# Dealing rows to partitions so that the DMA engines of one core work on neighbouring blocks of DRAM

## The chip, the cores and the metric

One NeuronCore of one Trainium2 chip runs the kernel; the other cores are idle. The metric is the time of one execution in device microseconds. Runs of the kernel before lie within 3725.8 to 3726.7 us.

## The reference

A residual add and an RMS norm over 65536 rows of 2048 float32:

```python
batch, seq, dim = 32, 2048, 2048
z = x + residual
rms = np.sqrt(np.mean(z ** 2, axis=-1, keepdims=True) + eps)
return (z / rms * gamma).astype(np.float32)
```

It reads two arrays of 537 MB and writes one of 537 MB.

## The kernel before

The 65536 rows go through SBUF in 74 tiles: one of 128 x 3 rows, one of 128 x 5, then 72 of 128 x 7. A tile costs three transfers, all issued from the SP queue: load the residual (`r_area`), load x (`z`), store the result (`out`, from `z`). Partition p holds 7 rows that follow one another in DRAM, a block of 56 KiB.

```python
    def rows(t, i):
        k = sizes[i]
        return t[starts[i] : starts[i] + P * k, :].rearrange("(p r) m -> p r m", r=k)
    # ... cut ...
    def load_x(sp, t, d=0):
        i = t.i + d
        inc(sp.dma_start(out=z[i % 2][:, : sizes[i], :], in_=rows(x_f, i)), "x_in", i)
    # ... load_r: the same with r_area and r_f; cut ...
    def sp_turn(sp, t):
        i = t.i
        t.wait(sp, "done", -1)                  # tile i-1 is scaled
        inc(sp.dma_start(out=rows(o_f, i - 1), in_=z[(i - 1) % 2][:, : sizes[i - 1], :]),
            "s_out", i - 1)
        # ... cut ...
        t.wait(sp, "add_a")                     # first part of the add of tile i is done
        load_r(sp, t, 1)
        t.wait(sp, "s_out", -1)                 # the store has landed, its z is free
        # ... the last tile is loaded in four pieces; cut ...
        load_x(sp, t, 1)
```

VectorE adds and scales, ScalarE squares and sums; both work on whole partitions and don't care which rows a partition holds.

## Time and profile before

| | before |
|---|---|
| time | 3726.47 us median of 4 (3725.92 to 3726.7) |
| bytes moved | 1610.66 MB, 432 GB/s over the span |
| a packet of 56 KiB on one DMA engine | 2.116 to 2.128 us from fastest to 99th per cent |
| VectorE, ScalarE busy | 62%, 29% |

The page's lines stand in the prediction below, with how they are read. A packet is one engine's copy of one contiguous run; here, one partition's block. The packet durations come from the trace's packet records, which hold start, length and size, but neither engine nor address. So which engine serves which partitions is nowhere recorded. The engines are numbered here by the group that they serve; their own numbers are not in the records.

### The profile page before, as it was taken

Reading aid. Unit: us, or ns where it says so; the run is one execution under the profiler, and the core shown is the slowest. Engines: PE = TensorE matmul, PEld = TensorE weight load, DVE = VectorE, ACT = ScalarE, POOL = GpSimd, SP = SyncE. Lnnn points to the kernel's source line nnn. Section 1 sums busy time; section 2 is a strip of 40 time slices with the busy share of each in tenths; the row PEclk is TensorE's granted clock in tenths of the full one; section 3 lists DMA queues with packets and bytes.
Section 4 is the critical chain, followed back from the end, with each engine's and each line's share of the span. In section 5 each row is a group of like instructions: output and inputs, shape, how many; then the busy total and the mean of one; then the engine's idle time right before and its main releaser. Section 6 shows DMA issues by size and latency. Waiting matters only on the chain.

```text
span 3724.7 us, 3652 instructions
## 1 busy us (share of the span) xinstructions
DVE 2302.5 (62%) x816; ACT 1072.4 (29%) x1176; POOL 0.2 (0%) x4
## 2 busy tenths in 40 slices
DVE  5666665566665566665566665566665566655566
ACT  2233322233322233322233322233322233322233
POOL 0000000000000000000000000000000000000000
DMA  9999999999999999999999999999999999999999
GB/s 420 432 434 434 434 434 434 432 434 434 435 434 434 434 434 436 434 434 434 433 434 434 434 434 434 434 434 434 434 434 434 434 434 434 434 434 434 434 434 398
DMA packets 32964, 1610.69 MB, mean 432 GB/s; under 512 B 3712, under 2 KB 3776, under 8 KB 3776
## 3 DMA queue, kind: packets, MB, share of 16 engines
q1 hardware_dynamic: 32960, 1610.66, 99.9%
q14 instruction: 4, 0.03, 0.0%
HBM read 1073.77 MB, written 536.87 MB: 432 GB/s over the span
## 4 chain that ended last, share of the span: by engine, by line
DMA 66%; DVE 22%; issue 9%; ACT 2%; SPq 0%; DVEq 0%; ACTq 0%
DMA out_dram<-z 33%; DMA z<-in_x_dram 33%; DVE z L170 15%; DVE z L175 7%; ACT sq_junk L221 1%; DMA r_area<-in_gamma_dram 0%; ACT rms L229 0%; DVE rstd L195 0%; DVEq L126 0%; SPq L255 0%; DVE r_area L274 0%; ACTq L209 0%; ACTq L126 0%; DVE tail_rstd L291 0%; SPq L160 0%
## 5 line engine op out<-in xcount | busy, mean ns | idle before, releaser
L170 DVE TENSOR_TENSOR z<-z,r_area 128x8192 f32<-128x8192 f32 (+2 forms) x150 | 1109.4, 7437 | 1253.2 <-DMA z<-in_x_dram 1227.6
L221 ACT ACTIVATE sq_junk<-z 128x2048 f32<-128x2048 f32 x512 | 963.4, 1882 | 2618.1 <-DVE z L170 2606.7
L175 DVE SCALAR_TENSOR_TENSOR z<-z,rstd,gamma_tile 128x2048 f32<-128x2048 f32 x505 | 1153.5, 2344 | 5.2
L195 DVE RECIPROCAL rstd<-rms 128x4 f32<-128x4 f32 (+2 forms) x146 | 25.3, 173 | 130.8 <-ACT rms L229 130.8
L221 ACT ACTIVATION_READ_ACCUMULATOR sq_junk<-z 128x1 f32 x512 | 95.4, 186 | 0.0
L229 ACT ACTIVATE rms<-ssq,eps_tile 128x4 f32<-128x4 f32 (+2 forms) x146 | 43.3, 297 | 13.4
L175 DVE SCALAR_TENSOR_TENSOR z<-z,tail_rstd,gamma_tile 128x2048 f32<-128x2048 f32 x7 | 16.2, 2346 | 0.1
L276 DVE LOAD_MASK_SELECT gamma_tile<-r_area x1 | 0.0, 14 | 16.4 <-DMA r_area<-in_gamma_dram 16.4
L276 DVE STREAM_SHUFFLE gamma_tile<-r_area 128x2048 f32<-128x2048 f32 x1 | 2.3, 2290 | 0.0
L274 DVE MEMSET r_area<- 128x2048 f32 x1 | 1.8, 1765 | 0.4 <-issue 0.4
L221 ACT ACT_TABLE_LOAD x1 | 1.3, 1283 | 0.9 <-SPq L75 0.9
L229 ACT ACT_TABLE_LOAD x1 | 1.3, 1283 | 0.1
L229 ACT ACTIVATE tail_rms<-tail_ssq,eps_tile 128x2 f32<-128x2 f32 (+1 forms) x4 | 1.2, 296 | 0.1
L273 DVE MEMSET eps_tile<- 128x1 f32 x1 | 0.1, 59 | 1.0 <-SPq L75 1.0
L291 DVE RECIPROCAL tail_rstd<-tail_rms 128x2 f32<-128x2 f32 (+1 forms) x4 | 0.6, 158 | 0.0
L348 POOL MEMSET const-bfloat16-1.0<- 128x1 bf16 x1 | 0.1, 102 | 0.0
L348 POOL MEMSET const-uint8-127<- 128x1 uint8 x1 | 0.1, 102 | 0.0
L348 POOL MEMSET const-float32-1.0<- 128x1 f32 x1 | 0.1, 99 | 0.0
L348 POOL MEMSET const-float32-0.0<- 128x1 f32 x1 | 0.1, 98 | 0.2 <-issue 0.2
## 6 DMA issues: line engine op xcount, KB each, us to landing
r_area<-in_residual_dram SPq DMA_DIRECT2D x72, 7168.0 KB, 27.2
z<-in_x_dram SPq DMA_DIRECT2D x71, 7168.0 KB, 33.8
out_dram<-z SPq DMA_DIRECT2D x71, 7168.0 KB, 34.5
z<-in_x_dram SPq DMA_DIRECT2D x3, 2048.0 KB, 26.3
out_dram<-z SPq DMA_DIRECT2D x3, 2048.0 KB, 13.9
r_area<-in_residual_dram SPq DMA_DIRECT2D x1, 5120.0 KB, 25.3
z<-in_x_dram SPq DMA_DIRECT2D x1, 5120.0 KB, 36.8
out_dram<-z SPq DMA_DIRECT2D x1, 5120.0 KB, 24.7
```

Source lines behind the costliest of these rows:

```text
L170: return v.tensor_add(out=s, in0=s, in1=r_area[:, e + a : e + b, :])
L175: ins = v.scalar_tensor_tensor(out=s, in0=s, scalar=rs[:, c + g - a : c + g - a + 1], in1=gamma_tile[:, :], op0=mult, op1=mult,)
L195: v.reciprocal(out=rstd[p][h][:, :n], in_=rms[p][h][:, :n]).then_inc(dve, U)
L221: s.activation(out=sq_junk[:, :], in_=src[:, g, :], func=Act.Square, accum_out=sq[:, g - a : g - a + 1],)
L229: return s.activation(out=rm, in_=sq[:, : b - a], func=Act.Sqrt, bias=eps_tile[:, :], scale=inv_d)
L273: v.memset(eps_tile[:, :], float(eps))
L274: v.memset(stage, 0.0).then_inc(tail_ev["add"], 1)
L276: v.stream_shuffle(gamma_tile[:, :].rearrange("p (a b) -> p a b", a=16), stage, [0] * 32)
L291: v.reciprocal(out=tail_rstd[:, a:b], in_=tail_rms[:, a:b]).then_inc(dve, U)
L348: nc = _bacc.Bacc("TRN2", target_bir_lowering=False, num_devices=1)
```

## The change

The intent: while the 16 DMA engines work through a transfer, they should be on neighbouring blocks of DRAM. The rows of a tile are dealt so that block number 16j + e goes to partition 8e + j; if engine e serves partitions 8e to 8e+7, the 16 engines start on blocks 0 to 15, then go on to 16 to 31.

```diff
     def rows(t, i):
         k = sizes[i]
-        return t[starts[i] : starts[i] + P * k, :].rearrange("(p r) m -> p r m", r=k)
+        t = t[starts[i] : starts[i] + P * k, :]
+        return t.rearrange("(j e r) m -> e j r m", e=16, r=k)
# ... cut: two index expressions for the pieces of the last tile get one more dimension
```

Loads and stores use the same `rows`, so every row comes back to its place.

More of the change, by code (lines that the diff above doesn't have):

```diff
@@ L160, in sp_turn @@
                 sp.dma_start(
-                    out=z[last % 2][:, a:b, :], in_=rows(x_f, last)[:, a:b, :]
+                    out=z[last % 2][:, a:b, :], in_=rows(x_f, last)[:, :, a:b, :]
                 ).then_inc(x_tail[k], U)
@@ L265, in sync_program @@
             sp.dma_start(
-                out=rows(o_f, last)[:, a:b, :], in_=z[last % 2][:, a:b, :]
+                out=rows(o_f, last)[:, :, a:b, :], in_=z[last % 2][:, a:b, :]
             ).then_inc(s_tail, U)
```

## The prediction

The point is 6300 us, with a range of 3780 to 7480 us: 1.7 x 3711 + 15 = 6324, where 3711 us is the bytes at the measured 434 GB/s and 15 us is start and end. 2 for a pair of engines in step (2 x 2.12 = 4.24 us a packet) and 1.7 as the centre stand as estimates. A pair means two engines that hold each other up; that there are such pairs p1 shows, further below.

> **What bounds the kernel now.** I read the page from the top: busy engines, the slices, the queue, then the groups with their idle time, then the waits of the queue that issues the transfers, and last one stretch of the chain of waits.
>
> The busy shares and the slices (40 equal stretches of the span, DMA being the mean busy tenths of the 16 engines):
>
> ```profile
> span 3724.7 us, 3652 instructions
> ...
> DVE 2302.5 (62%) x816; ACT 1072.4 (29%) x1176; POOL 0.2 (0%) x4
> ...
> DMA  9999999999999999999999999999999999999999
> GB/s 420 432 434 434 434 434 434 432 434 434 435 434 434 434 434 436 434 434 434 433 434 434 434 434 434 434 434 434 434 434 434 434 434 434 434 434 434 434 434 398
> ...
> q1 hardware_dynamic: 32960, 1610.66, 99.9%
> ```
>
> No compute engine is near full, and the 16 DMA engines are busy for 99.9% of the span. Except in the first and last slice the rate stands at 434 GB/s, flat. [...] Per engine it is 434 / 16 = 27.1 GB/s. The bytes alone take 1610.66 MB / 434 GB/s = 3711 us, which leaves about 15 us of the 3726.35 us for start and end.
>
> Who waits (groups: busy and mean, then idle time before and its releaser) and what one transfer takes:
>
> ```profile
> L170 DVE TENSOR_TENSOR z<-z,r_area 128x8192 f32<-128x8192 f32 (+2 forms) x150 | 1109.4, 7437 | 1253.2 <-DMA z<-in_x_dram 1227.6
> ...
> r_area<-in_residual_dram SPq DMA_DIRECT2D x72, 7168.0 KB, 27.2
> z<-in_x_dram SPq DMA_DIRECT2D x71, 7168.0 KB, 33.8
> out_dram<-z SPq DMA_DIRECT2D x71, 7168.0 KB, 34.5
> ```
>
> VectorE's only large idle time is for x to land. A 7 MiB transfer needs 7.34 MB / 434 GB/s = 16.9 us of service, yet lands 27 to 34.5 us after issue: it stands in the ring behind about one whole other transfer. So the rings don't run dry. A stretch of the chain of waits in the middle of the run (start, length, what) says the same, two transfers' time per link:
>
> ```profile
> 978.42 34.42 DMA out_dram<-z
> ...
> 1012.86 33.81 DMA z<-in_x_dram
> ```
>
> A tile is three transfers, 50.8 us, against 2302.5/75 = 31 us of VectorE. The bound is the rate at which 16 DMA engines pass bytes, and nothing else has a say.
>
> How the bytes are cut: 228 of the 232 transfers carry tiles. 228 x (128 + 16) = 32832, plus four small gamma loads of 16 + 16 packets, is exactly 32960. So each partition's run of a tile (7 rows, 56 KiB) is one packet, 8 per engine and transfer, and each engine adds one completion write. In the trace's packet records a 56 KiB packet takes 2.116 to 2.128 us from the fastest to the 99th per cent, that is 27.1 GB/s, whether it is a read or a write of DRAM.
>
> [...]
>
> **The change part by part.** No computation changes, nor the number of transfers, their bytes or the waits. The listing of the built program against the old one shows only the shapes of the transfers moved: where both sides had 128 rows of 14336 elements, the DRAM side is now 16 x 8 x 14336 and the SBUF side 128 x 1 x 14336. Runs stay 56 KiB long, so 128 + 16 packets per transfer stay.
>
> Removed on the DRAM side: distance. I expect this to be worth nothing. If each engine is at a fixed 27.1 GB/s, DRAM is not what it waits for. [...]
>
> Added on the SBUF side, and not intended: [...]
>
> Its cost in lockstep: [...] a packet 4.24 us instead of 2.12, a 7 MiB transfer 33.9 us instead of 16.9, the run 2 x 3711 + 15 = 7437 us. Compute at 31 us a tile hides under 101 us.
>
> What softens it: [...] So the size hangs on the lag within pairs. In the landing records of the kernel before, the 16 landings of one transfer lie 0.9 to 1.1 us apart from first to last in the first 100 us, and mostly 3.3 to 4.7 us later. In packets of 2.12 us that is 0.5 at first and 1.6 to 2.2 later, for the most distant engines; a pair is usually closer. [...] I take 1.7 as the centre: 1.7 x 3711 + 15 = 6324, rounded to 6300 us.
>
> Issue of a transfer takes 0.33 us on the queue's sequencer in the timeline; a three-dimensional shape may take longer. Even 0.3 us more over 228 issues is 68 us, but beside at least 17 us of queued transfers it is hidden, so 0.
>
> **The rivals.**
>
> (1) Nothing happens: [...] The time would be 3726 give or take 10 us.
>
> (2) The pairs unlock themselves: [...] The time would be near 3750 to 4000. [...]
>
> (3) DRAM gains: a rate over 434 GB/s. Against: the ceiling above[...].
>
> (4) Neighbouring blocks make DRAM slower, all 16 engines being close together. I give it little. It would show as slow packets with no doubling pattern.
>
> **Range and chances.** Full lockstep is the upper end, 7437[...]. The lower end, 3780, holds most of the self-unlocking case but not the nothing-happens case. I give 16% to within 2% (rival 1, and a quick complete unlocking), 1% to faster, 83% to slower. Within slower, about a sixth lies below 4300, the rest spread from 5000 to 7450. The point is the middle of an uneven distribution, not a sharp value.
>
> **What would show it.** Right: the same 32960 packets and 1610.66 MB on the queue, DMA still at 9 in every slice (engines count as busy while blocked), GB/s well under 434, packets of 56 KiB taking between 2.12 and 4.24 us with many near the upper value, landings of 7 MiB loads stretched by the same factor, busy times of VectorE and ScalarE unchanged in us but a smaller share. GB/s rising along the span would show lag building up. Wrong: 434 GB/s throughout[...], packets longer than 4.3 us[...] (DRAM), or DMA share falling below 9 with the queue's waits on issue grown (issue cost).

## The result, and the profile after

The changed kernel takes 7070.9 us, median of 4 (7038.2 to 7098.18), against 3726.47 us. The ratio is 1.8972, with a 95% interval of 1.8868 to 1.9075. Ratios here are the mean time of one kernel's fast runs over that of the other's of the same rounds, so not quite the ratio of the medians quoted.

The page of the changed kernel, in the parts that answer to those of before: busy engines, slices, queue, the group that waits, and the transfers with their median time to landing.

```profile
span 7044.8 us, 3652 instructions
...
DVE 2302.6 (33%) x816; ACT 1072.4 (15%) x1176; POOL 0.2 (0%) x4
...
DMA  9999999999999999999999999999999999999999
GB/s 227 239 233 228 234 232 234 231 232 225 229 231 228 228 227 223 229 229 230 229 222 226 228 229 228 225 222 228 229 229 228 223 228 229 230 229 225 223 228 241
...
q1 hardware_dynamic: 32960, 1610.66, 99.7%
...
L171 DVE TENSOR_TENSOR z<-z,r_area 128x8192 f32<-128x8192 f32 (+2 forms) x150 | 1109.4, 7437 | 4544.6 <-DMA z<-in_x_dram 4544.6
...
r_area<-in_residual_dram SPq DMA_DIRECT2D x72, 7168.0 KB, 56.6
z<-in_x_dram SPq DMA_DIRECT2D x71, 7168.0 KB, 68.4
out_dram<-z SPq DMA_DIRECT2D x71, 7168.0 KB, 91.8
```

Packets and bytes are the same to the last one, and so is what VectorE and ScalarE do, in us. What changed is that the engines, busy as before (99.7%), pass half as much: 229 GB/s. Busy here means that an engine has a packet open, not that it moves bytes at its full rate; only GB/s beside the busy share shows the difference. VectorE's wait for x grew from 1228 to 4545 us, by 3317 us, which is nearly the whole of the added 3344 us. The rate is flat from the first slice to the last. The median landing times did not stretch by one factor: 2.08 and 2.02 times for the two loads, 2.66 times for the store.

In the packet records the mean packet of 56 KiB went from 2.118 to 4.012 us. The distribution between 1000 and 3000 us of the run:

```
                before      after
under 2.2 us      100%         7%
2.2 to 4.1 us       0%        18%
over 4.1 us         0%        75%   (median of all 4.30, 90th per cent 4.47)
```

The timeline shows an issue of a transfer on SP taking 0.54 to 0.59 us where it took 0.33: the three-dimensional shape costs about 0.22 us more per issue, beside transfers that take over 30 us.

### The profile page after: what moved, and what is told of

It is laid out like the page before. It is cut to its first block, busy times and chain, and to the rows that moved or that the text cites. A ratio compares the mean times of both kernels' runs of the same rounds, so it can differ in the third digit from the quotient of the medians.

```text
span 7044.8 us, 3652 instructions
## 1 busy us (share of the span) xinstructions
DVE 2302.6 (33%) x816; ACT 1072.4 (15%) x1176; POOL 0.2 (0%) x4
## 3 DMA queue, kind: packets, MB, share of 16 engines
q1 hardware_dynamic: 32960, 1610.66, 99.7%
## 4 chain that ended last, share of the span: by engine, by line
another core or an unknown queue 64%; DVE 23%; issue 9%; ACT 2%; DMA 1%; DVEq 0%; ACTq 0%; SPq 0%
DVE z L171 16%; DVE z L176 7%; ACT sq_junk L222 1%; DMA z<-in_x_dram 1%; DMA r_area<-in_gamma_dram 0%; ACT rms L230 0%; DVE rstd L196 0%; DVEq L280 0%; DVEq L127 0%; DVE r_area L275 0%; SPq L256 0%; ACTq L210 0%; ACTq L127 0%; SPq L141 0%
```

## The experiments

The theory, which no run up to here shows: with a DRAM side of 16 x 8 (the straight deal: group e to partitions 8e to 8e+7) the engines e and e+4 are a pair, and each of them gets half of its rate while they are in step. The rivals: neighbouring blocks in DRAM are slow; the three-dimensional shape is; the straight deal slows every engine. In the expectations the numbers that stand under no rival's name, up to p1, are those of this theory.

### e1: neighbouring blocks, in groups of four partitions

```diff
-        return t.rearrange("(j e r) m -> e j r m", e=16, r=k)
+        return t.rearrange("(j c r) m -> c j r m", c=32, r=k)
```

Block 32j + c now goes to partition 4c + j: 32 groups of four partitions instead of 16 of eight. Blocks that follow one another still go to different groups and the shape stays three-dimensional, but the deal isn't the straight one. Which blocks are worked on at a time isn't recorded, here or in e2; near and far follow from the order of the blocks in the program.

> The DRAM side keeps the neighbouring blocks of the changed kernel (32 groups by 4 instead of 16 by 8[...]), and the transfer stays three-dimensional[...]. [...] the loss goes, about 3726 us, 434 GB/s, packets of 2.12 us. Rival 'neighbouring blocks in DRAM are slow': it stays near 7070 us, or at least well over 5000. Rival 'a three-dimensional shape is dealt or issued slowly': it stays near 7070 us as well. If DRAM distance is worth anything at all, this run shows it as a difference of a few tenths of a per cent from the kernel before.

Measured: 3727.39 us, median of 5; ratio to before 1.0005, interval 0.9991 to 1.0018. Packets 2.116 us. The slices of its page:

```profile
GB/s 415 432 433 433 435 432 435 434 433 434 433 433 434 433 434 433 434 434 435 434 434 433 433 433 433 433 433 433 433 435 433 433 435 433 433 433 433 434 435 398
```

Back at the old rate, 433 to 435 GB/s in most slices. So neither the neighbourhood in DRAM nor the shape is what costs, and neither gains anything: the intent of the change, reached without its side effect, is worth nothing within 0.2%.

### e2: blocks far apart, but the straight deal

```diff
-        t = t[starts[i] : starts[i] + P * k, :]
-        return t.rearrange("(j e r) m -> e j r m", e=16, r=k)
+        # cut: the first two tiles stay as in the changed kernel
+        h = i % 2     # two tiles share a stretch
+        t = t[starts[i - h] : starts[i - h] + 2 * P * k, :]
+        return t.rearrange("(e h j r) m -> h e j r m", e=16, h=2, r=k)[h]
```

> The blocks of DRAM that the engines read at a time lie 896 KiB apart (each engine walks through 8 neighbouring blocks[...], from a run of 16), but the DRAM side has 16 as its slowest dimension[...]. [...] about 7070 us, 6900 to 7200, 229 GB/s. Rival 'neighbouring blocks in DRAM are slow': about 3726 us.

Measured: 7054.59 us, median of 4; ratio 1.8968 (1.8871 to 1.9065), the changed kernel's to within 0.1%. With e1 the four corners are filled: near or far makes no difference, the deal makes all of it.

### e3 and e4: only the loads, only the stores

Both give wrong rows.

```diff
 # e3: stores by the old function, loads by the new one; e4: the other way round
-            sp.dma_start(out=rows(o_f, i - 1), in_=...)
+            sp.dma_start(out=rows_old(o_f, i - 1), in_=...)
```

> Wrong result on purpose: loads as in the changed kernel, stores as in the kernel before, so rows land in wrong places. Loads are 2/3 of the bytes. [...] 3711 x (2/3 x 1.9 + 1/3) + 15 = 5950 us. If only writes into SBUF (loads) suffer: 7070 minus nothing, that is near 7000 cannot be, it would be 3711 x (2/3 x 2.35 + 1/3), the same total as the changed kernel, 7070. If only reads out of SBUF (stores) suffer: 3726 us.

> Wrong result on purpose: stores as in the changed kernel, loads as in the kernel before. Stores are 1/3 of the bytes. [...] 3711 x (2/3 + 1.9/3) + 15 = 4840 us. If only writes into SBUF suffer: 3726 us. If only reads out of SBUF suffer: 7070 us. The excess of this run and of e3 over 3726 us should add up to that of the changed kernel, 3344 us, if the two parts are independent.

Measured, one run each: e3 6397.07 us, e4 4499.35 us. Stretches of the two, first e3, then e4 (us, busy us, clock, DMA share, GB/s):

```profile
1000.00:6000.00 5000.00, 1790.49 (x627) 832.96 (x912) 0.00 (x0) 1.00 1.00 251
```

```profile
1000.00:4000.00 3000.00, 1539.21 (x539) 716.05 (x784) 0.00 (x0) 1.00 0.99 358
```

The excesses over before are 2671 and 773 us, together 3444, close to the changed kernel's 3344: both directions suffer, nearly independently. But not equally. With 15 us outside, loads run at (6397 - 15 - 1237) / 2474 = 2.08 times their old service time, stores at (4499 - 15 - 2474) / 1237 = 1.62 times. My expectation of 1.9 for both missed by 450 and 340 us. A factor above 2 isn't in a theory where the two engines of a pair get half of their rate each, without loss; in that theory a factor of 1.6 needs a lag. Both are followed up below.

### e5 to e8: setting a lag within pairs in the changed kernel

If the two engines of a pair are 4 packets apart, they should be out of each other's way. That was the estimate, and so is the factor of 2 - d/4 for a lag of d packets behind the 1.5 below. For stores p2 and p3 bear out its end (with a lag of 4, 2.12 us a packet and 419 GB/s). Extra copies from DRAM to DRAM in the second turn (into rows that the last tile overwrites later) are meant to hold back some engines.

```diff
         load_r(sp, t, 1)
+        if i == 2:
+            for e, c, n in [(12, 0, 2), (4, 2, 4)]:      # e5: (16, 0, 2), (16, 2, 4)
+                sp.dma_start(out=rows(o_f, last)[:e, c:n], in_=rows(r_f, last)[:e, c:n]
+                ).then_inc(s_lag, U)
         t.wait(sp, "s_out", -1)
# e7, e8: four copies of 4 groups each, issued by GpSimd: 4 (2) packets of 56 KiB, 4 of 512 B, twice
```

> Control: in turn 2 of the changed kernel, two extra copies from DRAM to DRAM (into rows that the last tile overwrites) give each of the 16 engines 4 more packets of 56 KiB. No engine gains on another. Lag theory: the lag within pairs stays, so 7070 plus some 10 to 20 us, within 7000 to 7150.

> As the control, but one copy whose slowest dimension is 12 and one whose slowest dimension is 4, 2 packets per engine each, issued from the same queue. If a copy with slowest dimension k runs on the first k engines, engines 0-3 come 2 packets behind 4-7, and 8-11 come 2 behind 12-15[...]. Lag theory with a lag that stays: factor 2 - 2/4 = 1.5, so about 5580 us. If the lag decays (engines that run ahead run dry and restart together): back at about 7000, with only the slices after the copies faster. Rival without phases[...]: no change from the control, 7000 to 7150.

> The same idea with all pairs 4 packets apart and a total spread of 4: four copies issued by GpSimd with slowest dimension 4 (4 packets of 56 KiB, 4 of 512 B, 4 of 56 KiB, 4 of 512 B)[...] if the delayed ones are not one of each pair, nothing happens. Lag theory with a lag that stays: near 3726 to 4300 us[...]. If the lag decays: fast slices (up to 434 GB/s) right after the copies, then back to about 230 GB/s, total 6500 to 7070. Rival without phases: 7000 to 7150 and no fast slice.

> As the previous one with 2 packets instead of 4: all pairs 2 apart, spread of 2. Lag theory with a lag that stays: factor 1.5, about 5580 us. If it decays: a stretch near 290 GB/s after the copies, then back to about 230. Rival without phases: 7000 to 7150.

Measured, one run each: 7119.85, 7071.04, 7088.31 and 7043.19 us. Three lie within the spread of the changed kernel, the control 0.7% over its median; the hoped-for lag did nothing that lasts. Stretches of e7 (its copies run from 168 to 223 us):

```profile
150.00:200.00 50.00, 31.41 (x11) 14.62 (x16) 2.49 (x4) 1.00 1.01 282
200.00:300.00 100.00, 31.41 (x11) 14.61 (x16) 0.00 (x0) 1.00 0.99 243
300.00:400.00 100.00, 31.41 (x11) 14.61 (x16) 0.00 (x0) 1.00 1.00 228
```

The 282 GB/s is not a gain: the copies themselves move 1.85 MB, and the changed kernel without them has 249 GB/s from 150 to 200 us, 1.65 MB less. Taken alone, this speaks for the rival without phases. It can't decide: whether the GpSimd copies held back the intended engines isn't recorded, and the kernel's waits may have undone the lag. So I took the kernel away.

### p1: the deals by themselves

A program that only transfers, in packets of 56 KiB. Each way to deal is three rounds of three transfers in a row:

```python
def phase(e, j, b, store, lag=0):         # e engines, j partitions each, from partition b
    for rep in range(3):
        if lag: ...                        # a small transfer on engines 0-3 first
        for k, buf in enumerate([a_buf, b_buf, c_buf]):
            w = buf[b : b + e * j, :, :]
            d = dram(o_f if store else x_f, e, j, 7)     # "(j e r) m -> e j r m"
            go(k, d if store else w, w if store else d)
        settle()
```

> Transfers alone, no computation, wrong result on purpose: ten ways to deal packets of 56 KiB, each as three rounds of three transfers in a row, first as loads, then as stores. 'a x b' is a engines with b packets each, engine e serving partitions be to be+b-1. [...] the old deal 434 GB/s; 16 x 8 about 210; 4 x 8 [...] 108 GB/s, all packets 2.12 us; 5 x 8 adds engine 4[...]: three fifths of the packets at 2.12 us, two fifths at 4.3 us; 8 x 8 all at 4.3 us, 105 GB/s; 8 x 4 on partitions 0-31 and on 64-95 both all at 2.12 us, 217 GB/s; 16 x 4 all at 4.3 us, 210 GB/s. [...] Rival 'the straight deal[...] slows everything': 4 x 8 and 8 x 4 slow as well. Last, 8 x 8 once more with a small transfer ahead that holds only engines 0-3 back by 2, then by 4 packets, with no wait in between: if the lag stays, factor 1.5 and 1.0 (about 145 and 217 GB/s once both run); if the pair locks again by itself, 105 GB/s as without it. Stores: by the split of the loss between loads (2.08 times) and stores (1.6 times), the shared deals should be slowed less than loads, 16 x 8 about 270 GB/s.

Packet records of one of the three rounds of each (GB/s from the first packet's start to the last one's end, share of packets under 2.2 and over 4.0 us, mean in us):

```
                         loads                           stores
deal            GB/s  <2.2  >4.0  mean         GB/s  <2.2  >4.0  mean
old deal         421   96%    0%  2.15          431  100%    0%  2.13
16 x 8           208    0%   98%  4.39          215    3%   79%  4.08
4 x 8            107   96%    0%  2.15          107   96%    0%  2.14
5 x 8             66   57%   35%  3.01           67   57%   33%  2.98
8 x 8            104    0%   96%  4.39          107    3%   80%  4.14
8 x 4, 0-31      210   92%    0%  2.17          216  100%    0%  2.12
8 x 4, 64-95     208   92%    0%  2.17          216  100%    0%  2.12
16 x 4           204    0%   96%  4.43          207    0%   98%  4.39
8 x 8, lag 2     125   12%   43%  3.57          126   32%   46%  3.42
8 x 8, lag 4     151   48%    6%  2.62          178   81%    4%  2.31
```

The same in stretches of the profile, loads of 4 x 8, 5 x 8, 8 x 8, lag 2 and lag 4 (us, POOL busy, clock, DMA share, GB/s):

```profile
555.30:606.90 51.60, 0.00 (x0) 1.00 0.25 107
766.90:870.50 103.60, 0.00 (x0) 1.00 0.21 65
1082.90:1188.50 105.60, 0.00 (x0) 1.00 0.50 104
1736.30:1828.40 92.10, 0.00 (x0) 1.00 0.49 125
2012.80:2091.60 78.80, 0.00 (x0) 1.00 0.45 151
```

The second line is the telling one. A fifth engine is added, and the transfer takes twice as long (103.6 us, not 51.6) although three of the engines have finished by half of it: a share of 0.21 is two engines busy throughout and three for half, (2 + 1.5) / 16 = 0.22. The fifth engine collides with one other and no more; which one isn't recorded. 4 x 8 and 8 x 4, on partitions 0-31 and on 64-95, run at full speed (2.12 to 2.17 us a packet), which ends the rival that the straight deal slows every engine. And the partitions tell who collides: 8 x 4 on partitions 0-31 takes 2.17 us a packet as loads and 2.12 as stores; 16 x 4, which adds 32-63, takes 4.43 and 4.39, and it isn't the number of engines, since 16 by the old deal take 2.15 and 2.13. A lag helps, for loads (104 to 125 and 151 GB/s) and for stores (107 to 126 and 178). So the pairs and the phase are real; what the kernel does to the lag is the next question. One expectation missed: stores of 16 x 8 reached 215 GB/s and not 270 (p2 shows why a round of three transfers is too short for that).

### p2: does a lag survive waits?

```python
for t in range(24):
    if t >= back:
        sp.wait_ge(*landed[t - back])      # back = 3, 2, 1
    go(...)
```

> Transfers alone, wrong result on purpose: does a lag within pairs survive waits? Streams of 24 transfers of the 8 x 8 deal[...], started with engines 0-3 held back by 4 packets, where transfer n is issued after the landing of n-3, then n-2, then n-1; then the stream with n-3 without the lag; then 16 x 8 with n-2 where only engines 0-3 are held back and the pairs 8/12 to 11/15 are in step. First loads, then stores. Theory 'engines that run dry restart together, and are in step again': with n-3 and n-2 the lag of 4 packets stays (an engine may run 16 or 8 packets ahead), packets near 2.5 us as loads and 2.1 us as stores, about 170 to 210 GB/s of the 217 that eight engines can do; with n-1 the ring runs dry at each transfer, all packets 4.3 to 4.4 us, about 100 GB/s. Without the lag: loads 104 GB/s flat, stores slowly rising from 107 as they drift apart. 16 x 8: the lower half soon waits for the upper half, runs dry and falls into step: after a few transfers near 210 GB/s as loads, no better than the same deal without a lag. If instead lags vanish for another reason, n-3 and n-2 fall back to 104 within the stream.

Stretches, loads first (lag 4 with a wait for n-3, n-2, n-1; no lag with n-3; 16 x 8 with only the lower pairs apart), then the same as stores (the third lines begin with the second transfer of their stream):

```profile
68.50:540.90 472.40, 0.00 (x0) 1.00 0.49 188
543.00:1026.30 483.30, 0.00 (x0) 1.00 0.49 184
1066.40:1926.60 860.20, 0.00 (x0) 1.00 0.47 98
1929.10:2769.60 840.50, 0.00 (x0) 1.00 0.50 105
2771.80:3621.30 849.50, 0.00 (x0) 1.00 0.99 208
```

```profile
3623.20:4045.60 422.40, 0.00 (x0) 1.00 0.50 211
4047.40:4469.40 422.00, 0.00 (x0) 1.00 0.49 211
4504.90:5352.30 847.40, 0.00 (x0) 1.00 0.47 99
5354.00:5909.50 555.50, 0.00 (x0) 1.00 0.48 159
5911.20:6577.00 665.80, 0.00 (x0) 1.00 0.96 266
```

Two transfers ahead are enough to keep a lag over all 24 transfers (184 to 211 of 8 x 27.1 = 217 GB/s); with one, nothing is issued beyond the transfer under way, and the lag is gone from the second transfer on (98 and 99). The fourth lines show the difference of e3 and e4 again: without any help stores drift apart (159, and in the packet records the mean falls from 4.12 us in the first 100 us to 2.14 us in the fifth), while loads stay in step (105, flat). The fifth line of the loads contradicts the theory of pairs alone: engines 0-3 were held back as in the first line, yet in the packet records only 12 of the 3072 packets of that stretch are under 2.2 us, all in its last 7 us, when only a few engines still had work. Before an engine could run out of issued packets there is none. The lag was there all the same: of the 16 completion writes of the first transfer (packets of 4 bytes), four come 15 us after the other twelve.

### p3: which pairs have to be apart

The changed kernel's own deal, 16 x 8, in streams of 20 transfers, with lags set by copies from DRAM to DRAM.

> Transfers alone, wrong result on purpose: streams of 20 transfers of the changed kernel's own deal, 16 x 8, first loads, then stores; lags are set by copies from DRAM to DRAM[...] on the first 12 or the first 4 engines. In order: no lag; every pair 4 packets apart (engines 0-3 behind by 8, 4-7 and 8-11 by 4), transfer n issued after n-3 landed; the same after n-2; only the pairs of the upper eight engines 4 apart; only those of the lower eight; every pair 2 apart. In the last probe, 16 x 8 loads with only the lower pairs apart stayed at 208 GB/s from the first transfer on, although 8 x 8 with the same lag ran near full rate. Theory 'a pair in step also holds up engines outside it, as loads': every pair apart gives well over 300 GB/s with n-3; either half alone apart stays near 210 as loads; as stores a half apart helps, 260 or more. Theory 'pairs only': a half apart gives fast packets in that half until it runs dry, visible as a share of packets near 2.1 us in the first 100 us, also as loads. With n-2 and a spread of 8 packets the front engines run dry, so the lag should shrink and the rate fall below that with n-3. If every pair apart stays near 210 too, the lag of pairs does not explain the changed kernel's loads[...].

Loads: no lag; all pairs 4 apart with n-3; the same with n-2; only the upper pairs apart; only the lower; all 2 apart. Then stores: no lag and all pairs 4 apart.

```profile
67.70:774.50 706.80, 0.00 (x0) 1.00 1.00 208
777.10:1286.30 509.20, 0.00 (x0) 1.00 0.99 296
1288.40:1811.20 522.80, 0.00 (x0) 1.00 0.99 288
1813.40:2528.00 714.60, 0.00 (x0) 1.00 1.00 209
2530.30:3235.80 705.50, 0.00 (x0) 1.00 1.00 209
3237.90:3947.80 709.90, 0.00 (x0) 1.00 1.00 209
```

```profile
3949.70:4450.10 500.40, 0.00 (x0) 1.00 0.97 293
4452.10:4811.30 359.20, 0.00 (x0) 1.00 0.98 419
```

As stores, with all pairs apart, the straight deal runs at 419 GB/s, all but the old rate. The stores not shown missed my expectation: a half apart (292 and 293) or all 2 apart (295) is no better than no lag, which drifts apart by itself (293). As loads, it gets to 296 at best (I had expected well over 300), and only if all pairs are 4 apart; half of them apart, or all of them 2 apart, change nothing. In the packet records of the fourth stream fast packets occur in the first 8 us only, while the copies that set the lag still run. After them there is none, although three transfers of 8 packets per engine are issued ahead, 24 x 2.12 = about 51 us of work at full rate. Running out of packets can't be the reason; as loads, pairs in step hold up engines outside the pair.

"4 apart" and "2 apart" count packets of the copies. The lag that they left can be read from the completion writes of the first loads. Between the two engines of a pair it is about 7.6 us with the lower pairs apart and 13.5 us with the upper, 1.7 and 3.1 of the slow packets that follow; with all "2 apart" it is 3.3 to 4.8 us, one slow packet; with all "4 apart" 7.6 to 9.6 us, 2.5 to 3.1 packets of that stream. So a full lag of 4 was not reached as loads, and what it would give was not measured.

### p4: who holds up whom

The straight deal on the first 5, 8, 9, 12, 13 and 16 engines, then 12 and 16 with the lower pairs 4 apart. The first theory below is that only the two engines of a pair slow each other.

> Transfers alone, wrong result on purpose: which engines does a pair in step hold up, as loads? Streams of 9 transfers of the straight deal on the first 5, 8, 9, 12, 13 and 16 engines, then 12 with the lower pairs set 4 packets apart, then 16 with the same; loads first, then stores. With 5 engines 1-3 have no partner, with 9 engine 8, with 12 engines 8-11, with 13 engines 9-11. [...] share of packets near 2.1 us of 3/5, 0, 1/9, 1/3, 3/13, 0 in the streams without lag; with lag, 12 engines nearly all fast, 16 half fast until the front engines run dry after 24 packets (51 us or more). Theory 'a pair in step also holds up the engines eight numbers above it, as loads': 3/5, 0, 0, 0, 0, 0; with lag, 12 fast, 16 slow at once. As stores the first theory in both cases.

Loads of 8, 9, 12, 12 with lag and 16 with lag, then stores of 8, 9 and 12:

```profile
364.20:676.20 312.00, 0.00 (x0) 1.00 0.50 106
678.50:994.00 315.50, 0.00 (x0) 1.00 0.56 117
996.30:1311.50 315.20, 0.00 (x0) 1.00 0.74 157
...
1942.60:2131.00 188.40, 0.00 (x0) 1.00 0.70 268
2133.20:2454.40 321.20, 0.00 (x0) 1.00 0.99 208
```

```profile
2731.00:3005.20 274.20, 0.00 (x0) 1.00 0.47 119
3007.10:3282.70 275.60, 0.00 (x0) 1.00 0.51 134
3284.60:3559.50 274.90, 0.00 (x0) 1.00 0.61 179
```

Read the DMA share. With 12 engines, 8 to 11 have no partner in the theory, and as stores they run as if they had none, working half the time: 0.61, where (8 + 4 x 0.5) / 16 = 0.625. As loads they are busy all the time, 0.74 of at most 0.75, and move no more: they are slowed to the pace of the lower eight. In the packet records of the loads with 9 and with 12 engines no packet is under 2.2 us; with the lower pairs set apart, 55% are, and a single one of 880 is over 4 us. With 5 engines 55% are fast, so engines 1 to 3 aren't held up by the pair that the fifth is part of. Here the held-up engines are among the upper eight, held by the lower ones. It goes the other way too: the last line of the loads has the same lag in the lower pairs and adds engines 12 to 15, which puts the upper pairs in step, and after the copies no packet is fast until the last few us (208 GB/s; the fifth stream of p3 shows the same). Which engine holds up which was not tried; the theory of eight numbers apart is one guess.

## Why the prediction was right, point by point

**The bound.** Right. 434 GB/s is 16 times what one engine passes with no other in its way, to within 2%: 4 engines move 107 GB/s, 8 move 216 and 16 move 431 (stores of p1), and e1 reaches the same 434 GB/s with another order of DRAM addresses. What sets the rate of an engine, the runs don't tell.

**DRAM distance is worth nothing.** Right: e1 1.0005, e2 no different from the changed kernel.

**Pairs of engines in each other's way.** Right as far as the runs reach: p1's 4 x 8 against 5 x 8 (51.6 and 103.6 us), and the gain when engines 0-3 are held back against 4-7 (8 x 8 stores: 107 and 178 GB/s). What the two of a pair have in common, beyond the partitions that p1 tried, no run shows. The engine numbers themselves are not in the records.

**The cost in lockstep.** Right in kind, too small in size. I took 4.24 us for a packet; as loads in step they take 4.35 to 4.43 us in the mean (p1: 16 x 8, 4.39), 3 to 4% more. So a sign that I had named for DRAM being slow, packets longer than 4.3 us, came true for 55% of the packets of the changed kernel; e1 and e2 show that DRAM was not the cause, and the sign was drawn too close to my own 4.24. Had everything stayed in step, 2.08 x 3711 + 15 = 7734 us would have come out, above the range that I gave. That 7071 lies in it is owed to the stores, which I had not treated apart: luck, as far as the range goes.

**The lag.** This is the step that failed, and with it the point of 6300 us: the factor 1.7 was mis-sized, it measured 1.90. I took the spread of the 16 landings of a transfer (0.5 to 2.2 packets) for the lag within pairs, with the same small lag for loads and stores. (The estimate 2 - d/4 makes 1.45 to 1.6 of the 1.6 to 2.2 packets of most of the run; 1.7 leaned towards lockstep.) In the changed kernel that spread is 17 to 24 us for nine transfers of ten (median 20 us), more than four packets, and yet three quarters of its packets are over 4.1 us: the spread of all landings doesn't tell how fast a pair runs. Whether the pairs themselves stayed in step there, or were apart and held up by others, isn't recorded. The estimate 2 - d/4 fits the end of its range: stores with lag 4 settle at 2.12 us (p2, after 100 us) and near full rate (p2, p3). In between it was tried only roughly: with "lag 2" the mean was 3.42 us as stores and 3.57 as loads (p1) where d = 2 gives 3.18. It fails for loads on 16 engines, where lags of one to three packets within pairs gave 209 GB/s as no lag does, unless all pairs were about three apart. The factor of 1.90 is made of 2.08 on two thirds of the bytes and 1.62 on one third: (2 x 2.08 + 1.62) / 3 = 1.93, near the measured 1.897. That rise of GB/s along the span which I named as a sign of lag building up didn't come.

**The rivals.** "Nothing happens" and "DRAM gains" fell with the result, "DRAM is slower" with e1 and e2. "The pairs unlock themselves" is true of stores left to themselves (p2: after some 400 us), and not of loads. That the factor of 1.62 of the kernel's stores comes from a part of that is likely, but not shown.

**Issue time.** Right: 0.22 us more per issue, hidden; e1 has the same kind of shape and takes 3727 us.

What stays open: why packets in step lose another 3 to 4% (as stores too: 4.39 us in p1's 16 x 4), why stores drift apart and loads don't, and by what path each half of the engines is held up by pairs in step of the other half as loads. In e5 to e8 two reasons for the missing effect are shown to exist (loads gain only with all pairs far apart: 296 GB/s in p3, otherwise 209; waiting for the transfer before ends the lag: 98 and 99 GB/s in p2), but which of them acted in each wasn't measured.

## What to carry to other kernels

The order of rows within a transfer is free for the computation, but the shape of the DRAM side isn't free: 16 groups of 8 nearly doubled the time (7070.9 us), while 32 groups of 4 (3727.39 us), or 128 on both sides (3726.47 us), kept the full rate. If the DMA busy share stays at 9 while GB/s halves, put packet durations beside the rate, and think of engines that wait for each other as well as of DRAM: the busy share alone can't tell the two apart, e1 and e2 did. Before optimising distances in DRAM, ask whether every engine already passes what it passes alone: here it did (27.1 GB/s, 2.116 us for a packet of 56 KiB), and there was nothing to win (e1: 1.0005).
